# Indexer scores of two heads in two 64-row halves of the matrix engine, and one gate tile moved

## The chip, the cores and the metric

The kernel runs on one core of a Trainium2 chip. The metric is the device time of one execution in microseconds; three runs of the kernel before gave 1056.82, 1057.84 and 1059.62 us, median 1057.84. The engines are PE (matrix multiply), DVE (vector), ACT (scalar), POOL (general) and SP (issues DMAs). PE writes into PSUM; ACT and DVE read PSUM and write SBUF.

## The reference, cut to what matters

One layer of a streaming encoder, for 1024 prompt tokens and 32 sample tokens. One input projection gives, among others, the indexer's queries `qi` (8 heads of 64), its keys `ki` (64), its head weights `wi`, and two merge gates. The indexer scores every pair of query and key, and attention then uses only the best keys of each query:

```python
logits = jnp.einsum('bthd,bsd->bths', qi.astype(f32), ki_all.astype(f32)) * (IDX_DIM ** -0.5)
score = jnp.einsum('bth,bths->bts', wi.astype(f32), jax.nn.relu(logits))
...
top_val, top_idx = lax.top_k(score, n_sel)
```

Prompt queries see the keys up to the end of their 64-token chunk and select 256; sample queries see 512 cached keys and 32 new ones and select 136. All data are float32, and the scores decide which keys are taken, so they are computed in more than one pass of the matrix engine's rounded float32.

## The kernel before, in words

A float32 matrix is split into a high part (rounded to the engine's format) and a low part (the rest). A product then takes three passes: high by high, high by low and low by high. `mm3` (L270 to L272) does this for the projections.

**The stream.** All projections of 128 output columns are jobs of one stream `Z`. A job takes its weight tile (a DMA of 512 KB on SP), splits it in two (on ACT, DVE or POOL, as the job says), and issues 24 steps: three groups of 352 tokens by eight tiles of the contraction, each step one `mm3`. `run(us)` issues as many steps as fit into the given time at 0.483 us a step, so the order of PE's instructions is written by hand; a job's evacuation from PSUM follows its third group, in the selection some steps later (`LAG`). `gate_job(f)` is the job of gate tile f: its evacuation is a tanh on ACT (L707), and the result goes to DRAM with a DMA on SP. There are 16 gate tiles: 0 to NS-1 run at the start, NS to NI-1 behind the indexer's jobs, NI to 15 in the selection. With NS = NI = 7 none runs in the indexer.

**The indexer** (L1134 to L1194). Jobs: `ki`, then `qi0` to `qi3`, each of two heads. The evacuation of `qi` builds for each head a tile of 128 rows: 64 rows of the high part and 64 of the low part (L1127 to L1130), so that one pass over a key matrix that holds the keys twice gives high and low at once. For each of four pairs of heads, the seven query tiles (i = 2 to 7 of the prompt with 128(i+1) keys, and i = 8, the sample, with 32 queries and 544 keys), and each head: two passes (L1181 with the keys' high part, L1182 with the low part) in pieces of up to 512 columns into a PSUM tile `pss` of 1024 columns (two of these exist), a ReLU on ACT (L1184), and on DVE the weighted sum into `sco` (L1187, L1189). Then `run(0.25 + nk * FI)` issues stream steps. While pair j is scored, the stream projects `qi` of pair j+1; for the fourth pair it has nothing. The products of the merge's last gate row (L1109) come from a delay list in between. PE's order is by hand here; that of DVE, ACT, POOL and SP is found by the planner.

**The selection** (L1518 to L1621). 32 rounds of a binary search for the threshold of each query: ACT counts four of the tiles (L1513), DVE three (L1515), then DVE moves the thresholds (L1571, L1578). Each round issues `run(4.0)`. Behind the rounds the marks (L1585 to L1612, mostly DVE) write the masks `mb`, with further `run` calls. The stream has 16 jobs for this part: K, V and Q of the first pair of attention heads, gates 7 to 15 and `za0` to `za3`. The weight splits of the gates are on POOL here. `Z.until("za3")` at L1620 issues what is left of them. The order of DVE and ACT is by hand here too.

**The attention** follows: per item the products (L1349), maxima (L1355), exponentials (L1362), norm (L1367 to L1371), transposes (L1442 for rows, L1405 for the sample) and the output products, again with stream steps in between.

Of the kernel before, what the change touches and what calls it, by code (L numbers as in the profile page):

```python
# [7 lines left out]
F32 = mybir.dt.float32  # L8
F32R = mybir.dt.float32r
BF16 = mybir.dt.bfloat16  # L10
I32 = mybir.dt.int32
AF = mybir.ActivationFunctionType
ALU = mybir.AluOpType
# [4 lines left out]
NT = T + TS  # L18
# [5 lines left out]
NCH = 133  # L24
NST = 134
QT = [(i * 128, 128, 128 * (i + 1)) for i in range(8)]
NS, NI = 7, 7
WB = 5
SQ, HF, SM, GD, GH, NP, BL, HB, GL = 1, 4, 4, (1, 1, 0), 1, (0, 0, 2, 2), 1, 1, 0
TP = 1000  # L30
# [6 lines left out]
FI = 0.0007  # L37
# [20 lines left out]
def body(nc, tc, I, O, dbg=None):  # L58
# [3 lines left out]
    te, ve, se, ge, sp = nc.tensor, nc.vector, nc.scalar, nc.gpsimd, nc.sync  # L62

    def f32(ap):
        return ap.bitcast(F32)

    def split(h, l, src, heng, leng):
        if heng is se:
            se.copy(h, src)
        else:  # L70
            heng.tensor_copy(h, src)
        leng.tensor_sub(l, src, f32(h))  # L72
# [14 lines left out]
    def ps_x(tag, bufs, w=512):  # L87
        t = phase[1].tile([128, w], F32, tag=tag, bufs=bufs, name="ps" + tag)
        return t
# [14 lines left out]
    def ps_s(n="pss"):  # L104
        return ps_x("s", 2, 1024)
# [15 lines left out]
    def load_rows(xt, g, r, n, eng):  # L121
# [3 lines left out]
        if k < n:  # L125
# [30 lines left out]
                            op0=ALU.add, op1=ALU.mult)  # L156
# [109 lines left out]
    def wsplit(src, kt, n, pool=None, heng=None, leng=None):  # L266
        return wparts(wload(src, kt, n, pool), kt, n, pool, heng, leng)
# [52 lines left out]
    now, ve = ve, Later(ve, todo)  # L320
# [149 lines left out]
    for k in range(7):  # L470
        n = 1 << k
# [39 lines left out]
    ve = now  # L511
# [29 lines left out]
    ns = lambda n: slice(n * G3, (n + 1) * G3)  # L541
# [33 lines left out]
    class Stream:  # L575
# [77 lines left out]
        def run(self, us):  # L653
            self.credit += us / self.STEP
            while self.credit >= 1:
                if not self.step():
                    self.tick()
                self.credit -= 1
# [106 lines left out]
    for t in START.split():  # L765
# [6 lines left out]
        else:  # L772
            n = t.rstrip("0123456789")
# [210 lines left out]
    run = Z.run  # L984
# [77 lines left out]
    for q in range(4):  # L1062
# [4 lines left out]
        wh, wl = wsplit(w_glu[:, 128 * q:128 * q + 128], 4, 128, gp, leng=(ge, ve)[(YW >> q) & 1])  # L1067
        for n in range(3):
            c = ns(n)
            ps = ps_s("g")  # L1070
# [14 lines left out]
    sco = {i: scp.tile([128, 128 * (i + 1)], F32, name=f"sco{i}") for i in range(2, 8)}  # L1085
# [4 lines left out]
    ip = stI.enter_context(tc.tile_pool(name="ip", bufs=1, side="right", reuse_waits="tile"))  # L1090
# [28 lines left out]
    QS = {}  # L1119

    def qijob(j):
        def begin():
            qs = QS[j] = [ip.tile([128, NT], F32R, name=f"qis{e}", bufs=2) for e in range(2)]

            def ev(n, ps):
                c = ns(n)
                se.copy(qs[0][0:64, c], ps[0:64])  # L1127
                se.copy(qs[1][64:128, c], ps[64:128])
                ve.tensor_sub(qs[0][64:128, c], ps[0:64], f32(qs[0][0:64, c]))
                ve.tensor_sub(qs[1][0:64, c], ps[64:128], f32(qs[1][64:128, c]))  # L1130
            return ev
        return Job(f"qi{j}", wcol(C_QI + 128 * j), begin, heng=se, leng=ve)

# [18 lines left out]
    for k in range(9):  # L1152
        n = 128 if k < 8 else 32
# [9 lines left out]
    wi = cst.tile([128, 9, 8], F32)  # L1163
# [3 lines left out]
    kiH = ip.tile([128, 1568], F32R)  # L1167
    kiL = ip.tile([128, 1568], F32R)
    split(kiH, kiL, kid, ve, ge)
    for j in range(4):  # L1170
        Z.until(f"qi{j}")
        run(2.5)
        qs = QS[j]
        for i in range(2, 9):
            t0, m, k0, nk = (128 * i, 128, 0, 128 * (i + 1)) if i < 8 else (1024, 32, 1024, 544)
            for e in range(2):
                h = 2 * j + e
                ps = ps_s()
                for a in range(0, nk, 512):
                    b = min(nk, a + 512)  # L1180
                    te.matmul(ps[:m, a:b], qs[e][:, t0:t0 + m], kiH[:, k0 + a:k0 + b], start=True, stop=False)  # L1181
                    te.matmul(ps[:m, a:b], qs[e][:, t0:t0 + m], kiL[:, k0 + a:k0 + b], start=False, stop=True)  # L1182
                rl = ip.tile([128, 1024], F32, name="rl", bufs=2)
                se.activation(rl[:m, :nk], ps[:m, :nk], AF.Relu)  # L1184
                w = wi[:m, i, h:h + 1]
                if h == 0:
                    ve.tensor_scalar_mul(sco[i][:m, :nk], rl[:m, :nk], w)  # L1187
                else:
                    ve.scalar_tensor_tensor(sco[i][:m, :nk], rl[:m, :nk], w, sco[i][:m, :nk],  # L1189
                                            op0=ALU.mult, op1=ALU.add)  # L1190
                run(0.25 + nk * FI)
    for i in range(2, 8):
        ve.memset(sco[i][0:64, 128 * i + 64:128 * i + 128], -3.0e38)
    Z.flush()  # L1194
# [143 lines left out]
    class Soft:  # L1338

        def products(self, m, nk, mask, lhsT, rhs, np_=0):  # L1340
            self.m, self.nk, self.mask, self.np_ = m, nk, mask, np_
            self.P = at2.tile([128, 1024], F32, name="Sm", bufs=SM)
            self.S = []
            for a in range(0, nk, 512):
                c = slice(a, min(nk, a + 512))
                S = ps_x("s", 3)[:m, 0:c.stop - a]
                self.S.append((c, S))
                for t, r in enumerate(rhs):
                    te.matmul(S, lhsT, r[:, c], start=t == 0, stop=t == len(rhs) - 1)  # L1349
# [296 lines left out]
    for k in range(len(seq) + 3):  # L1646
        it = at(k)
        if k in first:
            p, begin = first[k]
            k0 = k  # L1650
# [9 lines left out]
        f = FA[p][e_] + FF * (it.i + 1 if it else 5)  # L1660
# [77 lines left out]
    for f in range(8):  # L1738
        wh, wl = wsplit(w_pa[:, 128 * f:128 * f + 128], 4, 128)
        tg = stg.tile([128, NT], F32, name="tgl", tag="stg")  # L1740
        sp.dma_start(tg, thD[8 + f])
        for n in range(3):
            ps = ps_x("m", 4)
# [63 lines left out]
    for rows in ((0, 1, 2), (8,), (3,), (4,), (5,), (6,), (LAST,)):  # L1807
        xts = {}
        for hcol in range(2):
            for i in rows:  # L1810
                n = 128 if i < 8 else 32
# [5 lines left out]
                for b_, c in enumerate(cols):  # L1817
                    ps = products(i, n, hcol, c)
# [4 lines left out]
                    if len(cols) == 2 and b_ == 0:  # L1823
                        ve.tensor_scalar(ss2[:n, 0, i:i + 1], ss2[:n, 0, i:i + 1], ss2[:n, 1, i:i + 1], None,
                                         op0=ALU.add)
# [53 lines left out]
```

## Time and profile before

| | |
|---|---|
| median of 3 runs | 1057.84 us (1056.82 to 1059.62) |
| profiled execution | 1056.18 us, of which span 1054.4 |
| PE busy | 994.8 us, 94% of the span |
| DVE busy | 761.5 us, 72% |
| ACT busy | 537.8 us, 51% |
| POOL busy | 260.2 us, 25% |
| granted PE clock, mean | 0.990 |
| score matmuls | L1181 and L1182, 96 each, 324.0 to 403.8 us |
| first projection of the selection | 404.19 us |
| first product of the attention | 609.84 us |

Times in rows are microseconds from the start of the span. A matmul's row shows its start, its length from first operand to last result, and its operands as rows by columns of the weights and shape of the stream; since matmuls are pipelined, the distance between two starts is what one costs, not its length. A row of a table of groups gives count, busy time and mean length in ns, then the idle time just before and what ended it.

### The profile page before, as it was taken

To read this page: it belongs to the slowest core of one execution; us is meant where nothing else is said; L and a number is where in the kernel's file an instruction comes from. 1 tells how busy PE (TensorE), PEld (TensorE's weight loads), DVE (VectorE), ACT (ScalarE), POOL (GpSimd) and SP (SyncE) were. 2 spreads that over 40 slices of the span, in tenths; PEclk is the share of its full clock that TensorE was granted. 3 is DMA by queue.
4 is the path that set the end of the run, shared out by engine and by line. 5 is a ranking of instruction groups with operands and counts; after the bars stand their busy time and mean duration, and the time that the engine had idled before them with its cause. 6 is when DMAs were issued, how large, how long until landed. Compare 5 with 4: busy or idle time off the path is not lost.

```text
span 1054.4 us, 17185 instructions
## 1 busy us (share of the span) xinstructions
PE 994.8 (94%) x6194; PEld 925.1 (88%) x6194; DVE 761.5 (72%) x1760; ACT 537.8 (51%) x1152; POOL 260.2 (25%) x471
## 2 busy tenths in 40 slices
PE   5999999998999989898999999999999999999997
PEld 3899999998889878898998998889898988998786
DVE  4669698994737789988889846756657776786534
ACT  3642245435435557768994346556556555443111
POOL 4200000313320231233313532333222231340000
PEclk9999999999899999999999999999999999999999
DMA  9923512317573110323232251242124622854311
GB/s 309 271 68 95 168 45 83 102 54 232 187 221 97 61 41 23 110 58 104 82 103 82 88 157 50 65 132 68 53 94 122 206 77 88 268 163 140 122 69 60
DMA packets 124177, 121.68 MB, mean 115 GB/s; under 512 B 14272, under 2 KB 104852, under 8 KB 124092
## 3 DMA queue, kind: packets, MB, share of 16 engines
q1 hardware_dynamic: 123712, 120.26, 37.2%
q8 instruction: 49, 0.80, 0.3%
q14 instruction: 36, 0.29, 0.1%
q10 hardware_dynamic: 220, 0.28, 0.1%
q0 software_dynamic: 160, 0.03, 0.0%
HBM read 85.64 MB, written 34.34 MB: 114 GB/s over the span
## 4 chain that ended last, share of the span: by engine, by line
PE 47%; DVE 10%; ACT 9%; issue 5%; POOL 0%; DMA 0%; POOLq 0%; ACTq 0%; DVEq 0%; SPq 0%
PE pz L270 6%; PE pz L272 6%; PE pz L271 6%; ACT junkb L1513 6%; PE pss L1349 3%; PE psm L1848 3%; PE psm L1850 3%; PE psm L1849 3%; PE pt L1442 2%; DVE junk L1515 2%; PE pspo L1461 2%; DVE sco L1189 1%; PE psm L270 1%; PE psm L272 1%; PE psm L271 1%
## 5 line engine op out<-in xcount | busy, mean ns | idle before, releaser
L270 PE MATMUL pz<-hH,wh 128*128 128x352 f32 (+1 forms) x776 | 261.5, 337 | 3.7 <-DVE zt L696 3.7
L272 PE MATMUL pz<-hH,wl 128*128 128x352 f32 (+1 forms) x776 | 251.5, 324 | 0.0
L271 PE MATMUL pz<-hL,wh 128*128 128x352 f32 (+1 forms) x776 | 251.5, 324 | 0.0
L263 POOL TENSOR_TENSOR wl<-raw,wh 128x256 fp32r<-128x256 f32 (+1 forms) x184 | 138.3, 779 | 135.5 <-ACT wh L258 128.1
L270 PEld LDWEIGHTS pz<-hH,wh 128*128 128x128 f32 (+1 forms) x776 | 145.9, 188 | 8.1 <-DVE zt L696 4.0
L271 PEld LDWEIGHTS pz<-hL,wh 128*128 128x128 f32 (+1 forms) x776 | 145.9, 188 | 1.3
L272 PEld LDWEIGHTS pz<-hH,wl 128*128 128x128 f32 (+1 forms) x776 | 145.7, 188 | 0.4
L1513 ACT ACTIVATE junkb<-sco,thr 128x896 bf16<-128x896 f32 (+3 forms) x128 | 103.6, 809 | 26.5 <-DVE thr L1578 20.1
L270 PE MATMUL pss<-hH,wh 128*128 128x352 f32 x304 | 102.4, 337 | 8.5 <-ACT tg L707 4.7
L272 PE MATMUL pss<-hH,wl 128*128 128x352 f32 x304 | 100.7, 331 | 1.2 <-POOL wl L263 1.2
L271 PE MATMUL pss<-hL,wh 128*128 128x352 f32 x304 | 100.5, 330 | 0.2 <-DVE hL L72 0.2
L1515 DVE TENSOR_SCALAR_CACHE_REDUCE junk<-sco,thr 128x1024 bf16<-128x1024 f32 (+2 forms) x96 | 96.9, 1010 | 2.4
L262 POOL CAST wh<-raw 128x256 fp32r<-128x256 f32 x88 | 35.0, 437 | 179.8 <-PE pz L271 164.2
L270 PEld LDWEIGHTS pss<-hH,wh 128*128 128x128 f32 x304 | 59.1, 194 | 11.6 <-POOL wh L262 5.3
L1445 DVE TENSOR_TENSOR PL<-pt,PH 128x512 fp32r<-128x512 f32 (+2 forms) x96 | 50.4, 552 | 25.8 <-ACT PH L1444 23.7
L1444 ACT CAST PH<-pt 128x512 fp32r<-128x512 f32 (+2 forms) x96 | 42.9, 482 | 46.1 <-PE pt L1442 43.4
L272 PEld LDWEIGHTS pss<-hH,wl 128*128 128x128 f32 x304 | 59.1, 194 | 1.7 <-POOL wl L263 1.7
L271 PEld LDWEIGHTS pss<-hL,wh 128*128 128x128 f32 x304 | 59.0, 194 | 0.4 <-DVE hL L72 0.4
L1362 ACT ACTIVATE Sm<-Sm,mx 128x128 f32<-128x128 f32 (+8 forms) x68 | 52.7, 775 | 9.2 <-DVE mx L1355 9.2
L1184 ACT ACTIVATE rl<-pss 128x384 f32<-128x384 f32 (+6 forms) x56 | 41.1, 738 | 29.8 <-PE pss L1182 21.5
L1189 DVE SCALAR_TENSOR_TENSOR sco<-rl,wi,sco 128x384 f32<-128x384 f32 (+6 forms) x49 | 46.4, 959 | 10.9 <-ACT rl L1184 10.0
L1850 PE MATMUL psm<-o,mL 128*128 128x512 f32 (+1 forms) x136 | 51.6, 381 | 0.0
(408 smaller groups left out, 2226.7 us busy)
## 6 DMA issues: line engine op xcount, KB each, us to landing
raw<-in_w_in SPq DMA_DIRECT2D x44, 512.0 KB
thD<-tg SPq DMA_DIRECT2D x16, 528.0 KB
tgl<-thD SPq DMA_DIRECT2D x16, 528.0 KB
wm<-in_w_mod SPq DMA_DIRECT2D x8, 1024.0 KB
rraw<-in_w_mod SPq DMA_DIRECT2D x4, 1024.0 KB
kd<-kd SPq DMA_DIRECT2D x32, 128.0 KB
xo<-in_x_prompt SPq DMA_DIRECT2D x8, 512.0 KB
rawo<-in_w_o SPq DMA_DIRECT2D x8, 512.0 KB
```

The costliest lines, as they stand in the source:

```text
L263: leng.tensor_sub(wl[:, c], raw[:, c], f32(wh[:, c]))
L270: te.matmul(ps, wh, xh, start=first, stop=False)
L271: te.matmul(ps, wh, xl, start=False, stop=False)
L272: te.matmul(ps, wl, xh, start=False, stop=last)
L1184: se.activation(rl[:m, :nk], ps[:m, :nk], AF.Relu)
L1189: ve.scalar_tensor_tensor(sco[i][:m, :nk], rl[:m, :nk], w, sco[i][:m, :nk], op0=ALU.mult, op1=ALU.add)
L1362: se.activation(P, P, AF.Exp, scale=-1.0, bias=self.mx, accum_out=self.rs)
L1444: se.copy(PH[:, b0:b1_, oc], src)
L1445: ve.tensor_sub(PL[:, b0:b1_, oc], src, f32(PH[:, b0:b1_, oc]))
L1513: se.activation(junkb[:m, :nk], x[:m], AF.Sign, bias=t, accum_out=cnt[:m, k:k + 1])
L1515: ve.tensor_scalar(junk[:m, :nk], x[:m], t, None, op0=ALU.is_lt, op1=ALU.add, accum_out=cnt[:m, k:k + 1])
L1850: te.matmul(ps, ml, wh, start=False, stop=last)
```

## The change

The queries are kept as a high and a low tile of two heads each (rows 0 to 63 are head 2j, rows 64 to 127 head 2j+1), split by one copy on ACT and one subtraction on DVE. A query tile is worked through in chunks of up to 512 columns (nk if it is at most 512, otherwise two halves). For each chunk there are three passes, high by high, low by high and high by low, and in each pass two matmuls: rows 0 to 63 into the first bank of the PSUM tile, rows 64 to 127 into the second. One ReLU takes both banks; DVE adds the two heads one after the other. `run` is called once a chunk, with the same sum over a pair of heads. NI becomes 8: gate tile 7 is projected behind `qi3`, with its splits on ACT and DVE, and no longer in the selection.

```diff
-NS, NI = 7, 7
+NS, NI = 7, 8
...
-            qs = QS[j] = [ip.tile([128, NT], F32R, name=f"qis{e}", bufs=2) for e in range(2)]
+            qh, ql = QS[j] = [ip.tile([128, NT], F32R, name=f"qi{h}", bufs=2) for h in "HL"]
 
             def ev(n, ps):
-                c = ns(n)
-                se.copy(qs[0][0:64, c], ps[0:64])
-                se.copy(qs[1][64:128, c], ps[64:128])
-                ve.tensor_sub(qs[0][64:128, c], ps[0:64], f32(qs[0][0:64, c]))
-                ve.tensor_sub(qs[1][0:64, c], ps[64:128], f32(qs[1][64:128, c]))
+                split(qh[:, ns(n)], ql[:, ns(n)], ps, se, ve)
...
-            for e in range(2):
-                h = 2 * j + e
-                ps = ps_s()
-                for a in range(0, nk, 512):
-                    b = min(nk, a + 512)
-                    te.matmul(ps[:m, a:b], qs[e][:, t0:t0 + m], kiH[:, k0 + a:k0 + b], start=True, stop=False)
-                    te.matmul(ps[:m, a:b], qs[e][:, t0:t0 + m], kiL[:, k0 + a:k0 + b], start=False, stop=True)
-                rl = ip.tile([128, 1024], F32, name="rl", bufs=2)
-                se.activation(rl[:m, :nk], ps[:m, :nk], AF.Relu)
...
-                run(0.25 + nk * FI)
+            w = nk if nk <= 512 else nk // 2
+            for a in range(0, nk, w):
+                ps = ps_s().rearrange("p (e c) -> p e c", e=2)[:m, :, 0:w]
+                kc = slice(k0 + a, k0 + a + w)
+                for x, (q_, k_) in enumerate(((qh, kiH), (ql, kiH), (qh, kiL))):
+                    for e in range(2):
+                        r = slice(64 * e, 64 * e + 64)
+                        te.matmul(ps[:, e], q_[r, t0:t0 + m], k_[r, kc], start=x == 0, stop=x == 2)
+                rl = ip.tile([128, 2, 512], F32, name="rl", bufs=2)[:m, :, 0:w]
+                se.activation(rl, ps, AF.Relu)
+                for e in range(2):
+                    h = 2 * j + e
+                    wh, dst = wi[:m, i, h:h + 1], sco[i][:m, a:a + w]
...
+                run((0.5 + 2 * nk * FI) * w / nk)
```

More of the change, by code (lines that the diff above doesn't have):

```diff
@@ L1172, in body @@
         run(2.5)
-        qs = QS[j]
+        qh, ql = QS[j]
         for i in range(2, 9):
             t0, m, k0, nk = (128 * i, 128, 0, 128 * (i + 1)) if i < 8 else (1024, 32, 1024, 544)
-            for e in range(2):
-                h = 2 * j + e
-                ps = ps_s()
-                for a in range(0, nk, 512):
-                    b = min(nk, a + 512)
-                    te.matmul(ps[:m, a:b], qs[e][:, t0:t0 + m], kiH[:, k0 + a:k0 + b], start=True, stop=False)
-                    te.matmul(ps[:m, a:b], qs[e][:, t0:t0 + m], kiL[:, k0 + a:k0 + b], start=False, stop=True)
-                rl = ip.tile([128, 1024], F32, name="rl", bufs=2)
[L1184 to L1190, printed above, removed]
-                run(0.25 + nk * FI)
+            w = nk if nk <= 512 else nk // 2
[11 more added lines that the diff above has]
+                    wh, dst = wi[:m, i, h:h + 1], sco[i][:m, a:a + w]
+                    if h == 0:
+                        ve.tensor_scalar_mul(dst, rl[:, e], wh)
+                    else:
+                        ve.scalar_tensor_tensor(dst, rl[:, e], wh, dst, op0=ALU.mult, op1=ALU.add)
+                run((0.5 + 2 * nk * FI) * w / nk)
     for i in range(2, 8):
```

## The prediction

> **What bounds the kernel now.** I read the page's totals first, then a table by stage cut where the PE's program changes: scores of the first three head pairs, scores of the fourth, the 32 rounds of the selection, the marks after them, the start of the attention.
>
> ```profile
> span 1054.4 us, 17185 instructions
> PE 994.8 (94%) x6194; PEld 925.1 (88%) x6194; DVE 761.5 (72%) x1760; ACT 537.8 (51%) x1152; POOL 260.2 (25%) x471
> ...
> PE 47%; DVE 10%; ACT 9%; issue 5%; POOL 0%; DMA 0%; POOLq 0%; ACTq 0%; DVEq 0%; SPq 0%
> ```
> ```profile
> 324.15:385.28 61.13, 60.94 (x355) 54.12 (x354) 47.47 (x64) 37.17 (x59) 9.35 (x12) 1.00 0.20 61
> 385.28:404.19 18.91, 15.32 (x64) 9.29 (x65) 18.50 (x27) 11.95 (x17) 5.76 (x7) 0.91 0.15 43
> 404.19:557.20 153.01, 142.02 (x872) 139.58 (x873) 134.33 (x326) 126.40 (x288) 43.08 (x81) 0.99 0.27 81
> 557.20:604.30 47.10, 45.05 (x270) 44.18 (x269) 44.01 (x68) 18.10 (x40) 23.58 (x26) 0.96 0.29 91
> 604.30:640.00 35.70, 34.57 (x226) 33.26 (x225) 17.64 (x52) 16.60 (x41) 10.05 (x21) 1.00 0.45 137
> ```
> The columns after the length are PE, weight loads, DVE, ACT and POOL busy, then the PE clock. PE has 94% of the span and the largest share of the chain, but not everywhere. Pairs 0 to 2 are PE's (60.94 of 61.13). Pair 3 is DVE's (18.50 of 18.91): no projection is left to run beside it, and weight loads wait for the ReLU to free PSUM:
>
> ```profile
> PEld pss L1181 <- ACT rl L1184: 7.9, 13, 1.4
> ```
> In the rounds DVE and ACT hand thresholds to each other and PE follows; in the marks DVE is full (44.01 of 47.10), and behind them PE still has projections to finish. A PE saving is worth its size only in the first stretch and from the marks on.
>
> **The change part by part.** First the PE's prices in the score stage: steps of the projection stream, and distance between starts by width.
>
> ```profile
> L270 PE MATMUL pz<-hH,wh 128*128 128x352 f32 x67 | 22.5, 335 | 0.0
> ```
> ```profile
> 324.15 0.34 PE L1181 MATMUL pss<-kiH,qis 128*128 128x384 f32 x1
> 324.33 0.34 PE L1182 MATMUL pss<-kiL,qis 128*128 128x384 f32 x1
> 324.50 0.32 PE L270 MATMUL pz<-hH,wh 128*128 128x352 f32 x1
> 324.66 0.32 PE L271 MATMUL pz<-hL,wh 128*128 128x352 f32 x1
> ...
> 331.54 0.32 PE L272 MATMUL pz<-hH,wl 128*128 128x352 f32 x1
> 331.79 1.07 PE L1109 MATMUL pg<-rraw,scP 128*32 128x512 f32 x8
> 332.78 0.43 PE L270 MATMUL pz<-hH,wh 128*128 128x352 f32 x1
> ...
> 340.01 0.39 PE L1181 MATMUL pss<-kiH,qis 128*128 128x512 f32 x1
> 340.24 0.40 PE L1182 MATMUL pss<-kiL,qis 128*128 128x512 f32 x1
> ```
> A 352-column matmul takes 0.16 us of PE, 384 columns 0.175, 512 columns 0.23, so width/2.4 ns and 16 ns on top. A step is three 352s: 0.483 us. The row product L1109 costs 1.1 us.
>
> *Scores, PE.* Stretch one holds 67 steps (32.4 us) and two L1109 (2.2 us); the other 26.5 us are three pairs of scores but for the sample tile of the last (about 1 us): **9.1 us a pair** for 48 matmuls. The new code has 12 chunks a pair (384, 512, and two each of 320, 384, 448, 512 and 272 columns), each with three passes by two halves. If the halves run side by side a pass costs one width: the twelve sum to 2.18 us, three passes to **6.5 us**. If not, 13.1.
>
> Do tiles of the array overlap? The trace has no two row halves. The nearest row is L1109: eight 512-column instructions into four column strips, each lasting about 0.6 us, in 0.99 us together. So strips overlap; I take that for row halves too.
>
> Each chunk is followed by at least one stream step, so PE goes from 128-row to 64-row tiles and back 48 times (about 46, the last ones lying together). The attention's sample item does this once a pair of heads, with five 64-row transposes; 72-row transposes are the comparison that stays in the full array:
>
> ```profile
> 754.29 0.32 PE L272 MATMUL pz<-hH,wl 128*128 128x352 f32 x1
> 754.54 0.51 PE L1405 MATMUL pt<-idf,Sm 64*128 64x64 f32 x5
> 754.99 0.43 PE L270 MATMUL pz<-hH,wh 128*128 128x352 f32 x1
> 755.25 0.32 PE L271 MATMUL pz<-hL,wh 128*128 128x352 f32 x1
> ```
> ```profile
> 313.17 0.32 PE L272 MATMUL pz<-hH,wl 128*128 128x352 f32 x1
> 313.33 0.42 PE L1158 MATMUL pt<-idf,zki 72*128 72x72 f32 x4
> 313.55 0.41 PE L270 MATMUL pz<-hH,wh 128*128 128x352 f32 x1
> 313.80 0.33 PE L271 MATMUL pz<-hL,wh 128*128 128x352 f32 x1
> ```
> From the matmul ahead to the second behind: 0.96 us with 64 rows, 0.63 with 72; a fifth transpose at 0.06 makes that 0.69. **A visit costs 0.27 us**, 0.09 of it at the entry (0.25 instead of 0.16). Bounds: 0 (the transposes are another data type) to 0.27; I take 0.27, since the entry wait precedes any difference in type. 46 visits: 12.4 us, more than the 4 x 2.6 = 10.4 us saved.
>
> The Trainium skill, TensorEngine Tiling (Array Packing), section Key Properties, says that a change of tiling mode drains the array; the rows agree. The same page's Theoretical Speedup gives up to 2x for a contraction of 64; by that alone the visits would be free and the pair 6.5 us.
>
> *Scores, DVE and ACT.*
>
> ```profile
> L1189 DVE SCALAR_TENSOR_TENSOR sco<-rl,wi,sco 128x896 f32<-128x896 f32 x7 | 8.1, 1158 | 1.7 <-ACT rl L1184 1.6
> ...
> L1130 DVE TENSOR_TENSOR qis<-pz,qis 64x352 fp32r<-64x352 f32 x11 | 5.8, 527 | 0.2
> ...
> L1189 DVE SCALAR_TENSOR_TENSOR sco<-rl,wi,sco 128x384 f32<-128x384 f32 x7 | 4.3, 613 | 1.3 <-ACT rl L1184 1.1
> ...
> L263 DVE TENSOR_TENSOR wl<-raw,wh 128x1024 fp32r<-128x1024 f32 x2 | 2.5, 1226 | 3.1 <-ACT wh L258 3.1
> ```
> From 384 to 896 columns: 1.064 ns a column and 0.2 us an instruction. DVE goes from 14 to 24 accumulations a pair, the columns unchanged: +2 us, +8 in all. Splitting qi takes one subtraction over 128 partitions instead of two over 64: -0.5 for each of nine evacuations inside the stage. The gate's weight split moves to DVE here: +1.2. DVE's 66.0 us of 80 (47.47 + 18.50) become about 70.7. ACT has 12 ReLUs a pair for 14 and half the qi casts; it gains the gate's cast and three tanh, and was busy 49 of 80, so nothing on the path. PSUM and SBUF tiles keep sizes and counts; a chunk still waits for the ReLU two chunks back, with the projection steps queued behind it on PE, and in stretch one that wait is almost nothing (0.19 us of PE not busy).
>
> *The gate tile.* 24 steps, 11.6 us of PE, leave the selection for pairs 2 and 3. Its weight load (SP), its two splits (POOL to ACT and DVE) and its store on SP go along; SP has nothing urgent behind it there (DMA share 0.15).
>
> *Sum for the stage.* 91 steps 43.9, three L1109 3.3, scores 26.1, visits 12.4: **85.7 us** from 324.15 to the first projection of the selection, which was 80.04 (404.19): **d = +5.7 us**.
>
> *Behind it.* By the code the rounds and marks ask for (128 + 46)/0.483 = 360 steps; the stream holds 16 tiles, 384. The remaining 24 run after the marks, and the gate's absence removes exactly these.
>
> ```profile
> 603.40 0.86 DVE L1594 TENSOR_TENSOR mb<-le,eq 32x544 bf16<-32x544 bf16 x1
> ```
> ```profile
> 609.84 0.22 PE L1349 MATMUL pss<-kH,qs 128*128 128x128 f32 x1
> 609.90 0.27 PE L1349 MATMUL pss<-kL,qs 128*128 128x128 f32 x1
> 610.01 0.38 PE L270 MATMUL pz<-hH,wh 128*128 128x352 f32 x1
> ...
> 616.42 0.27 PE L1442 MATMUL pt<-idf,Sm 128*128 128x128 f32 x1
> ```
> ```profile
> 610.60 0.52 DVE L696 SCALAR_TENSOR_TENSOR zt<-th,pz 128x352 f32<-128x352 f32 x1 [2.33 <-ACT th L695]
> 611.03 0.28 DVE L1355 CUSTOM_DVE_ANT_0 Sm<-pss,mb 128x128 f32<-128x128 f32 x1
> ...
> 612.97 0.54 DVE L1371 TENSOR_SCALAR Sm<-Sm,rs 128x128 f32<-128x128 f32 x1
> ```
> DVE ends the marks at 604.26 and starts the first maximum at 611.03, waiting for the last tile. With PE ahead, three 0.5 us evacuations move into the marks and one stays: the maximum at 606.3, 4.7 earlier. Its softmax is normalised at 613.51 and PE asks for it at 616.42: 2.9 more before PE waits. So PE's order moves by d - 11.6, DVE's lets it move by d - 7.6, and the later one decides: **d - 7.6 = -1.9 us**. The profiled execution took 1056.18 us (1.8 outside its span), 1.7 under the median 1057.84; from the median it is 1056.
>
> **The rivals.**
> 1. *The visits are cheap.* For it: the measured visit is of transposes. Then PE needs 73.3 us, but DVE's 70.7 with its waits becomes the bound; I take 75 to 77, d = -5 to -3, the end -13 to -11: 1045 to 1047, faster.
> 2. *Weights are not loaded ahead in halves.* The pair 609.90 to 610.01 shows 0.11 us where 128 columns of stream need 0.07: a load takes 0.11. Six loads in a row per chunk would be 0.66, over the matmuls by 0.9 us a pair: d = +9.3, end +1.7. If each half's load also waits for its own matmul, 0.11 a pass, 16 us in all, with the 0.09 entry in place of 0.27: d = +13.2, end +5.6, 1063; with 0.27 a visit besides, 1072. For it: the five transposes take 0.45 us, 0.09 each. The Trainium skill, TensorE: Matmul & The Clock Gate, Part 3, has such a rule: loads pass running matmuls only where the row groups differ. No row here shows two row groups.
> 3. *The halves do not overlap* (slower): 13.1 us a pair, 26 us more, d = +32, end +24; with free visits +12: 1070 to 1082. It decides from 1.9 + 3.2 = 5 us, so as soon as a fifth of the overlap is lost. Against it: L1109.
>
> **How the numbers follow.** Forecast (1053 to 1060) 0.41; rival 1 0.27; rival 2 beyond it 0.18; rival 3 0.12; other 0.02. About 3.2 us (0.3%) is what a measurement can tell from no change. Faster is rival 1 and 0.09 of the forecast: 0.36. Slower is rival 3, 0.12 of rival 2 and 0.02 of the forecast: 0.26. The rest, 0.38, is no change. The range takes in rival 1 and most of rival 2: 1046 to 1069.
>
> **What would show it.** The two matmuls of a pass starting within 0.05 us of each other and a pass repeating after 0.15 to 0.23 us: overlap. The first stream matmul after a chunk at 0.25 us or more, and a late first load: visits. The first projection of the selection at about 410; no stream left behind the marks; the first maximum at about 612. I am wrong if PE waits on DVE in all four pairs, or if the planner orders the ReLUs behind the gate's tanh.

## The result: 1071.6 us, 1.25% slower

The changed kernel takes 1071.6 us (median of 4 runs, 1069.98 to 1072.22); the kernel before, beside it, 1058.07 us (1056.82 to 1059.62). The ratio is 1.0125, 95% interval 1.0107 to 1.0143. The forecast was 1056 us, the range 1046 to 1069. The profiled execution took 1071.97 us with a span of 1070.2.

The page of the changed kernel: span, busy times, shares of the chain by engine.

```profile
span 1070.2 us, 17326 instructions
PE 1003.7 (94%) x6290; PEld 921.4 (86%) x6290; DVE 763.1 (71%) x1789; ACT 532.1 (50%) x1133; POOL 255.8 (24%) x463
...
PE 47%; DVE 11%; ACT 11%; issue 3%; POOL 1%; DMA 0%; ACTq 0%; POOLq 0%; DVEq 0%; SPq 0%
```

The totals say little: PE is 9 us busier, the other engines are within 6 us of before, and the mean granted clock is 0.974 for 0.990. The table by stage (after the length: PE, weight loads, DVE, ACT, POOL busy, then the PE clock) tells more. The rows are scores of pairs 0 to 2, scores of pair 3, rounds, marks, start of the attention.

```profile
325.82:395.28 69.46, 69.46 (x443) 49.63 (x442) 49.56 (x84) 34.21 (x46) 5.05 (x7) 1.00 0.18 54
395.28:419.80 24.52, 21.58 (x147) 14.84 (x145) 20.78 (x35) 12.87 (x19) 8.07 (x12) 0.96 0.14 44
419.80:576.30 156.50, 145.45 (x861) 142.88 (x862) 135.31 (x332) 126.70 (x288) 41.67 (x77) 0.95 0.28 84
576.30:623.50 47.20, 40.96 (x257) 40.65 (x255) 44.15 (x68) 16.59 (x38) 27.34 (x30) 0.96 0.32 103
623.50:656.00 32.50, 30.87 (x186) 29.55 (x187) 16.26 (x53) 15.74 (x38) 5.27 (x13) 0.91 0.34 101
```

The scores take 93.98 us instead of 80.04, and in pairs 0 to 2 PE is never idle (69.46 of 69.46): a gain for DVE or ACT is worth nothing there. In the marks PE is less busy than before, since the gate tile is gone, but neither rounds nor marks are shorter.

The 15.8 us of span split like this: 1.67 lie ahead of the first score (325.82 against 324.15; that point scatters from 323.9 to 328.9 over the kernels run here, and the change doesn't touch what precedes it), 13.94 in the scores, -1.01 from there to the attention's first row transposes (631.02 against 616.42), 1.20 behind them. The forecast was 0, +5.7, -7.6, 0. So two terms failed: the scores by 8, the selection by 6.6.

**The scores.** PE's timeline at the first chunk (start, length, line, operands; `x2` groups two neighbouring rows of one form, here both halves of a pass):

```profile
325.57 0.32 PE L272 MATMUL pz<-hH,wl 128*128 128x352 f32 x1
325.82 0.44 PE L1179 MATMUL pss<-kiH,qiH 64*128 64x384 f32 x2
326.10 0.34 PE L1179 MATMUL pss<-kiH,qiL 64*128 64x384 f32 x2
326.28 0.34 PE L1179 MATMUL pss<-kiL,qiH 64*128 64x384 f32 x2
326.55 0.43 PE L270 MATMUL pz<-hH,wh 128*128 128x352 f32 x1
326.81 0.32 PE L271 MATMUL pz<-hL,wh 128*128 128x352 f32 x1
```

From the second pass on, both matmuls of a pass lie in one row no longer than one alone (0.34), and the next pass starts 0.18 us later, one width. So the halves overlap. The price is at the borders: 0.25 into the chunk (0.16 within the stream), 0.28 from the first pass to the second (0.18 to the third), 0.27 from the last pass to the stream, 0.26 from that matmul to the next (0.16). From 325.57 to 326.81 are 1.24 us; less two 352s (0.32) and three widths (0.525) remain **0.39 us a visit**, not 0.27. Chunks of 512, 320 and 448 columns give 0.41, 0.39 and 0.40, those of the sample tile (32 columns of weights) 0.30. There are 44 visits (stretches of score matmuls between stream rows), eight of them of the sample tile: some 17 us. With 43.9 of stream, 3.3 of L1109, 26.1 of overlapped scores and the waits below (3.0) that is some 93 of the 93.98 us.

The weight loads of the same chunk (PEld) show what a visit is made of:

```profile
325.82 0.19 PEld L1179 LDWEIGHTS pss<-kiH,qiH 64*128 64x128 f32 x2 [0.22 <-issue]
325.93 0.19 PEld L1179 LDWEIGHTS pss<-kiH,qiL 64*128 64x128 f32 x2
...
326.54 0.19 PEld L270 LDWEIGHTS pz<-hH,wh 128*128 128x128 f32 x1 [0.25 <-issue]
326.65 0.19 PEld L271 LDWEIGHTS pz<-hL,wh 128*128 128x128 f32 x1
```

Within the stream a load starts about 0.16 us ahead of its matmul (L272's at 325.41 for 325.57). At both borders it starts only with its matmul (325.82, 326.54), and the next load follows 0.11 later. So each border costs twice: 0.09 until its first matmul starts, and 0.10 more until the second, about one load. In the sample tile's visits, whose weights have 32 columns, only the step from the first pass to the second is shorter: 0.15 for a width of 0.13. By these rows that part goes with the size of the weights. What holds the first load back isn't shown.

PE's waits in the scores (total us, times, longest):

```profile
PE pss L1179 <- ACT rl L1181: 1.9, 2, 1.5
PE pss L270 <- POOL qsm L1270: 1.1, 1, 1.1
```

**The selection.** PE's waits from 595 to 635 us, then the rows of PE and DVE around it:

```profile
PE pss L1347 <- DVE zt L696: 6.7, 1, 6.7
```
```profile
614.94 0.22 PE L1347 MATMUL pss<-kH,qs 128*128 128x128 f32 x1
...
616.93 0.32 PE L272 MATMUL pz<-hH,wl 128*128 128x352 f32 x1
624.00 0.58 PE L1347 MATMUL pss<-kH,qs 128*128 128x256 f32 x1 [6.75 <-DVE zt L696]
...
624.60 0.49 PE L270 MATMUL pz<-hH,wh 128*128 128x352 f32 x1
624.89 0.49 PE L271 MATMUL pz<-hL,wh 128*128 128x352 f32 x1
...
629.59 0.32 PE L270 MATMUL pz<-hH,wh 128*128 128x352 f32 x1
629.74 0.32 PE L271 MATMUL pz<-hL,wh 128*128 128x352 f32 x1
```
```profile
623.09 0.43 DVE L1592 TENSOR_TENSOR mb<-le,eq 32x544 bf16<-32x544 bf16 x1
623.45 0.50 DVE L696 SCALAR_TENSOR_TENSOR zt<-th,pss 128x352 f32<-128x352 f32 x1
623.88 0.50 DVE L696 SCALAR_TENSOR_TENSOR zt<-th,pz 128x352 f32<-128x352 f32 x1
624.31 0.27 DVE L1353 CUSTOM_DVE_ANT_0 Sm<-pss,mb 128x128 f32<-128x128 f32 x1
```

PE is ahead, as forecast: it issues the attention's first product at 614.94, 8.6 us before the last mark ends (623.52). But it can't issue the second. The attention's score tiles lie where the selection's wide tiles lay (`ps_z` takes the `s` tiles of the pool that `ps_phase` closes), and the last outputs of `za3` sit in them until DVE evacuates them, behind the last mark. Then PE runs at half clock (granted 0.50 from 624.0 to 629.3): 352 columns every 0.29 us instead of 0.16 for 15 matmuls, some 2 us more.

Of the 6.6 us by which the selection missed its forecast, 4.2 lie behind the first maximum, where these stops are: from there to the transposes are 6.71 us, and the forecast had 2.5 (5.39 less 2.9). The other 2.4 lie ahead of it. DVE's first mark, before and after:

```profile
557.57 0.75 DVE L1585 TENSOR_SCALAR le<-sco,thr 128x1024 bf16<-128x1024 f32 x1
```
```profile
575.23 0.76 DVE L1583 TENSOR_SCALAR le<-sco,thr 128x1024 bf16<-128x1024 f32 x1
```

It comes 155.43 us behind the first projection of the selection; in the kernel before it was 153.38. So the rounds, which the forecast left as they were, take 2.05 us more. DVE is no busier there (134.24 us for 134.63); it waits longer, 1.6 us for 0.5 on a DMA of K and 10.7 for 9.8 on ACT's counts. Why isn't shown. The marks are 1.6 us longer, as forecast for three evacuations that move into them.

### The profile page after: what moved, and what is told of

Its sections match the earlier page's. It is cut to its first block, busy times and chain, and to the rows that moved or that the text cites. A ratio compares the mean times of both kernels' runs of the same rounds, so it can differ in the third digit from the quotient of the medians.

```text
span 1070.2 us, 17326 instructions
## 1 busy us (share of the span) xinstructions
PE 1003.7 (94%) x6290; PEld 921.4 (86%) x6290; DVE 763.1 (71%) x1789; ACT 532.1 (50%) x1133; POOL 255.8 (24%) x463
## 4 chain that ended last, share of the span: by engine, by line
PE 47%; DVE 11%; ACT 11%; issue 3%; POOL 1%; DMA 0%; ACTq 0%; POOLq 0%; DVEq 0%; SPq 0%
PE pz L270 7%; ACT junkb L1511 7%; PE pz L271 6%; PE pz L272 6%; PE pss L1179 3%; PE pss L1347 3%; PE psm L1846 3%; PE psm L1848 2%; PE psm L1847 2%; PE pt L1440 2%; PE pspo L1459 2%; PE pspo L1457 1%; PE psm L270 1%; PE psm L272 1%; PE psm L271 1%
## 5 line engine op out<-in xcount | busy, mean ns | idle before, releaser
L270 PE MATMUL pz<-hH,wh 128*128 128x352 f32 (+1 forms) x792 | 271.4, 343 | 3.9 <-DVE zt L696 3.9
L272 PE MATMUL pz<-hH,wl 128*128 128x352 f32 (+1 forms) x792 | 257.5, 325 | 0.0
L271 PE MATMUL pz<-hL,wh 128*128 128x352 f32 (+1 forms) x792 | 257.5, 325 | 0.0
L263 POOL TENSOR_TENSOR wl<-raw,wh 128x256 fp32r<-128x256 f32 (+1 forms) x180 | 132.5, 764 | 145.9 <-ACT wh L258 138.6
L270 PEld LDWEIGHTS pz<-hH,wh 128*128 128x128 f32 (+1 forms) x792 | 149.6, 189 | 19.5 <-issue 12.6
L271 PEld LDWEIGHTS pz<-hL,wh 128*128 128x128 f32 (+1 forms) x792 | 149.8, 189 | 0.9
L272 PEld LDWEIGHTS pz<-hH,wl 128*128 128x128 f32 (+1 forms) x792 | 149.5, 189 | 0.4
L270 PE MATMUL pss<-hH,wh 128*128 128x352 f32 x288 | 99.2, 344 | 10.3 <-POOL wl L263 3.6
L272 PE MATMUL pss<-hH,wl 128*128 128x352 f32 x288 | 96.8, 336 | 0.2 <-POOL wl L263 0.2
L270 PEld LDWEIGHTS pss<-hH,wh 128*128 128x128 f32 x288 | 57.5, 200 | 13.4 <-POOL wl L263 3.9
L1188 DVE SCALAR_TENSOR_TENSOR sco<-rl,wi,sco 128x384 f32<-128x384 f32 (+4 forms) x84 | 55.9, 675 | 17.3 <-ACT rl L1181 16.0
L1181 ACT ACTIVATE rl<-pss 128x768 f32<-128x768 f32 (+4 forms) x48 | 39.9, 833 | 45.8 <-PE pss L1179 31.2
L1360 ACT ACTIVATE Sm<-Sm,mx 128x128 f32<-128x128 f32 (+8 forms) x68 | 52.7, 775 | 10.7 <-DVE mx L1353 10.7
L272 PEld LDWEIGHTS pss<-hH,wl 128*128 128x128 f32 x288 | 57.2, 199 | 0.5 <-POOL wl L263 0.5
L1353 DVE CUSTOM_DVE_ANT_0 Sm<-pss,mb 128x512 f32<-128x512 f32 (+4 forms) x68 | 40.2, 591 | 16.7 <-PE pss L1347 16.0
```

Of the source, the lines that this page charges most:

```text
L263: leng.tensor_sub(wl[:, c], raw[:, c], f32(wh[:, c]))
L270: te.matmul(ps, wh, xh, start=first, stop=False)
L271: te.matmul(ps, wh, xl, start=False, stop=False)
L272: te.matmul(ps, wl, xh, start=False, stop=last)
L1181: se.activation(rl, ps, AF.Relu)
L1188: ve.scalar_tensor_tensor(dst, rl[:, e], wh, dst, op0=ALU.mult, op1=ALU.add)
```

## The experiments

Theory T: (1) the halves overlap wholly; (2) a visit costs 0.39 us of a PE that is the bound; (3) the gate's work costs the scores more than it brings the selection, because held PSUM tiles stop PE there. It says nothing of the longer rounds. The rivals stand in the expectations. Positions are of the profiled execution, the ratio is to the kernel before:

| kernel | first score | first projection of the selection | first maximum | first row transposes | median us | ratio, 95% interval |
|---|---|---|---|---|---|---|
| before | 324.15 | 404.19 | 611.03 | 616.42 | 1058.07 | |
| changed | 325.82 | 419.80 | 624.31 | 631.02 | 1071.6 | 1.0125, 1.0107 to 1.0143 |
| e1 halves only | 326.68 | 416.41 | 623.98 | 629.37 | 1067.75 | 1.0087, 1.0063 to 1.0111 |
| e2 gate only | 324.29 | 410.23 | 613.71 | 619.72 | 1060.73 | 1.0020, 1.0006 to 1.0035 |
| e6 gate, MS | 324.47 | 410.40 | 614.96 | 616.35 | 1055.99 | 0.9968, 0.9945 to 0.9991 |
| e12 changed, MS | 325.92 | 419.88 | 624.78 | 626.16 | 1065.54 | 1.0077, 1.0064 to 1.0090 |

### e1 and e2: each part of the change alone

```diff
-NS, NI = 7, 8      # e1, from the changed kernel
+NS, NI = 7, 7
-NS, NI = 7, 7      # e2, from the kernel before
+NS, NI = 7, 8
```

> The two halves and three passes stay; the gate tile is put back into the selection (NS, NI = 7, 7). Theory T (each of the 46 switches between 64-row tiles and the 128-row stream costs about 0.39 us of PE, and the gate's 11.6 us of PE bring only some 2 to 3 us in the selection): the stage is 24 steps shorter than in the changed kernel, so from the first score matmul to the first projection of the selection about 82 to 84 us; the whole about 1062 to 1068 us. Rival R2 (it is the gate move that costs the time, the halves are about neutral): about 1058 us.

> The kernel before with only the gate tile moved (NS, NI = 7, 8). Theory T: the score stage about 5 us longer than the 80.04 us of before (it has idle PE that takes half of the 11.6 us), the selection 2 to 5 us shorter: 1057 to 1062 us. Rival R2 (the gate move costs the time): about 1070 us. If the selection gets 7 us shorter or more, the explanation by tiles that stay held is wrong, and it would be 1053 us or less.

Both are slower than before, e1 by 0.87%, e2 by 0.20%; together 1.07% of the 1.25%. R2 falls: most is the halves'. The score stage of e1 and of e2, and e1's waits of PE in it:

```profile
326.68:416.41 89.73, 80.91 (x514) 55.40 (x514) 68.05 (x118) 46.08 (x63) 12.93 (x18) 0.94 0.17 51
```
```profile
324.29:410.23 85.94, 84.44 (x490) 73.88 (x490) 68.04 (x91) 51.32 (x79) 13.29 (x15) 1.00 0.19 56
```
```profile
PE pss L1179 <- ACT rl L1181: 8.0, 8, 2.9
```

T had e1's stage at 82 to 84 us; it is 89.7. Without the gate's steps nothing runs beside the scores of pair 3, PE waits 8.0 us for the ReLUs, and the clock falls (0.94 over the stage). So moving the gate fills a gap that the halves make larger: its 11.6 us of PE lengthen the stage by 4.3 us in the changed kernel (93.98 against 89.73) and by 5.9 in the kernel before (85.94 against 80.04). In e2 the way from the first projection of the selection to the first row transposes shrinks by 2.7 us only (209.49 against 212.23), so the move alone loses.

### e3, e7, e8: the number of visits

```diff
-                run((0.5 + 2 * nk * FI) * w / nk)
+            run(0.5 + 2 * nk * FI)                          # e3: behind the last chunk of a tile

                     for e in range(2): ...                  # e7: also behind the first pass
+                    if x == 0:
+                        run((0.25 + nk * FI) * w / nk)
-                run((0.5 + 2 * nk * FI) * w / nk)
+                run((0.25 + nk * FI) * w / nk)

-                run((0.5 + 2 * nk * FI) * w / nk)
+                if i != 2 and b_ == nk:                     # e8: every two chunks; b_ = a + w
+                    run(0.5 + 2 * nk * FI + (0.5 + 768 * FI if i == 3 else 0))
```
(e8 also has MS = 0.0095, as e6 below.)

> The changed kernel, with the stream's turn taken once a query tile, behind its last chunk, in place of once a chunk: the same matmuls, ReLUs and accumulations, the same number of stream steps, but 28 visits to the 64-row tiles for 48. Theory T: 20 visits less at 0.39 us, the score stage about 7.8 us shorter than 94.0, the whole about 1064 us; some of it may come back as PE waiting for ReLUs between the two chunks. Rival R3 (the 24 accumulations a pair make DVE the bound of the stage): nothing gained, about 1071 us.

> The changed kernel, with each chunk's stream steps taken in two parts, one between the first and the second pass and one behind the third: 96 visits to the 64-row tiles for 48, all else the same. Theory T (0.39 us a visit): 48 x 0.39 = 18.7 us more in a stage that PE bounds, about 1089 us (1085 to 1092). Rival R6 (what e3 gained came from the grouping of the ReLUs and the stream, the switch itself costs the 0.27 us of the prediction or less): at most 13 us more, 1084 us or less; with a free switch about 1072 us.

> The changed kernel with a visit for every two chunks (24 for 48) and MS 0.0095. Theory T: from e3's 1062.3, four visits less at 0.39 us (1.6 us) and the 2 to 4 us that e6 is to gain: 1057 to 1059 us, the kernel before within its noise. If e6's step fails, about 1061 us; if PE waits for the ReLUs inside the longer visits, 1062 or more.

Measured: e3 1062.32 us (ratio 1.0047, 1.0031 to 1.0063), e7 1082.87 (1.0219, 1.0170 to 1.0269), e8 1058.48 (0.9998, 0.9975 to 1.0020). The score stage of each, in this order, each row from its own kernel's table:

```profile
324.85:412.21 87.36, 84.38 (x586) 65.67 (x586) 68.51 (x119) 46.40 (x66) 12.33 (x16) 0.99 0.18 55
```
```profile
326.64:432.31 105.67, 102.46 (x587) 63.88 (x586) 69.40 (x118) 47.10 (x64) 12.65 (x18) 1.00 0.15 46
```
```profile
328.92:414.66 85.74, 82.75 (x586) 65.95 (x586) 68.36 (x119) 45.93 (x66) 12.33 (x16) 0.99 0.19 56
```

The expectations count calls of `run`; where a call's credit is less than one step no visit ends. By the rows there are 27 visits in e3, 75 in e7, 23 in e8 and 44 in the changed kernel. So 31 more visits cost 11.69 us (105.67 less 93.98), 0.38 each; 17 fewer save 6.62, 0.39 each; 21 fewer save 8.24, 0.39 each. The price is the same from both sides and agrees with the rows. e7's total missed its range (1085 to 1092) because 17 of its 48 added calls make no visit. That total lies where R6 put it (1084 or less), but R6 reached it by 48 visits at 0.27; 31 visits at 0.27 would be 8.4 us, and the stage grew by 11.69, so R6 falls. R3 falls: with the same accumulations e3's DVE is about as busy as in the changed kernel (68.51 us for 70.34) and the stage is 6.6 us shorter. e8 came out as forecast (1057 to 1059), but its stage, 85.74 us, only draws level with the old scores beside the same gate tile (e2: 85.94).

### e4 and e5: do the halves overlap?

```diff
-                for x, (q_, k_) in enumerate(((qh, kiH), (ql, kiH), (qh, kiL))):
-                    for e in range(2):
+                for e in range(2):                          # e4: head by head
+                    for x, (q_, k_) in enumerate(((qh, kiH), (ql, kiH), (qh, kiL))):

-                        r = slice(64 * e, 64 * e + 64)
+                        r = slice(0, 64)                    # e5: both in the upper half
```

> The changed kernel with the six matmuls of a chunk ordered head by head (three passes of the upper half, then three of the lower) in place of pass by pass. Theory T (the two halves overlap wholly now): only the third pass of one head and the first of the other can still overlap, so a chunk takes five widths for three; over four pairs some 2 x 2.2 us x 4 = 17 us more, about 1089 us. Rival R4 (the halves hardly overlap even now): no change, about 1071 us.

> The changed kernel, with both matmuls of a pass reading the same 64 rows (the upper half; head 2j is computed twice and head 2j+1 left out). All else as in the changed kernel. Theory T (the halves overlap wholly, and head by head made no difference because a matmul of the other half is started past waiting ones): here nothing can overlap, so a chunk takes six widths for three, 6.5 us a pair more, 26 us in all on a PE that is the bound: about 1092 to 1102 us. Rival R4 (the halves don't overlap in the changed kernel either): no change, about 1071 us.

e4 took 1071.1 us (1.0122, 1.0101 to 1.0142): the number that R4 gave. Taken alone it would have buried the right theory. Its trace, and then that of e5, each for one chunk of 512 columns with the stream matmul behind it:

```profile
325.98 0.50 PE L1179 MATMUL pss<-kiH,qiH 64*128 64x512 f32 x2
326.32 0.39 PE L1179 MATMUL pss<-kiH,qiL 64*128 64x512 f32 x2
326.55 0.39 PE L1179 MATMUL pss<-kiL,qiH 64*128 64x512 f32 x2
326.87 0.44 PE L270 MATMUL pz<-hH,wh 128*128 128x352 f32 x1
```
```profile
326.83 0.72 PE L1179 MATMUL pss<-kiH,qiH 64*128 64x512 f32 x2
327.39 0.63 PE L1179 MATMUL pss<-kiH,qiL 64*128 64x512 f32 x2
327.86 0.63 PE L1179 MATMUL pss<-kiL,qiH 64*128 64x512 f32 x2
328.42 0.44 PE L270 MATMUL pz<-hH,wh 128*128 128x352 f32 x1
```

In e4 the two heads still run side by side, pass by pass, although the lower half's first matmul is issued behind all three of the upper half: 0.89 us a chunk. What failed is the premise that PE starts matmuls in the order of issue. In e5 both matmuls want the same 64 rows; a pass repeats after 0.47 us, two widths, and the chunk takes 1.59. The whole took 1093.88 us (1.0320, 1.0272 to 1.0367), inside T's range, and the stage:

```profile
324.44:442.29 117.85, 116.54 (x586) 87.56 (x586) 70.32 (x119) 47.32 (x64) 12.27 (x18) 0.99 0.14 41
```

23.9 us longer, where the forecast had 26 for the loss of the overlap. R4 falls.

### e6, e9 to e12: what stops PE behind the marks

```diff
-LAG, RS, MS, RM, RB = 4.0, 4.0, 0.008, 14.0, 1
+LAG, RS, MS, RM, RB = 4.0, 4.0, 0.0095, 14.0, 1     # e6, e10: on e2; e9: on before; e12: on the changed kernel
+LAG, RS, MS, RM, RB = 4.0, 4.0, 0.011, 14.0, 1      # e11: on e2
```

MS sets how much of the stream is issued among the marks; a larger one brings `za3`'s evacuations forward.

> The kernel before with the gate tile moved (as in e2) and MS 0.0095 for 0.008: the stream is drawn out earlier during the marks, so that the evacuations of the selection's last tiles are issued among the marks and their PSUM tiles are free when the attention's score products want them. Theory T (the gate's gain in the selection was lost because these evacuations, behind the marks, held the PSUM tiles of the attention's first products): PE's wait of 6 to 7 us there goes, and PE reaches the attention's first transposes 2 to 4 us sooner: 1057 to 1059 us for e2's 1060.7. Rival R5 (VectorE alone sets that point, its work is the same): no gain, about 1060.7 us.

> The kernel before with MS 0.0095 alone, the gate tile left in the selection. Theory T (e6 gained because PE had room and waited for held PSUM tiles; with the gate tile in the selection PE is the bound there and waits for nothing): no gain, 1056 to 1060 us. Rival R7 (the larger MS is a gain by itself, whatever the gate does): 4 to 5 us less than before, about 1053 us.

> The kernel of e6 once more, with more rounds, to see whether it beats the kernel before: 1054 to 1057 us, a ratio of about 0.997.

> As e6 with MS 0.011. In e6 VectorE goes from the last mark to the first maximum without a gap and PE still waits 3.5 us for one evacuation among the last marks. Theory T: that wait is shorter, but VectorE's own work now sets the first transposes (1.4 us behind the first maximum), so no more than 1 us is gained: 1054.5 to 1057 us.

> The changed kernel with MS 0.0095 alone. Theory T: the same held PSUM tiles cost the changed kernel what they cost e2, so it gains what e6 gained on e2 (4.7 us): about 1067 us (1065.5 to 1068.5). If the score stage had hidden something of it, less.

PE's waits behind the marks, first in e2, then in e6, and e6's PE rows behind the longer of them:

```profile
PE pss L1349 <- DVE zt L696: 6.8, 1, 6.8
```
```profile
PE pz L270 <- DVE zt L696: 3.5, 1, 3.5
PE pt L1442 <- DVE Sm L1371: 1.2, 1, 1.2
```
```profile
612.58 0.43 PE L270 MATMUL pz<-hH,wh 128*128 128x352 f32 x1 [3.53 <-DVE zt L696]
...
613.52 0.32 PE L270 MATMUL pz<-hH,wh 128*128 128x352 f32 x1
613.68 0.32 PE L271 MATMUL pz<-hL,wh 128*128 128x352 f32 x1
```
And DVE of e6 from its last evacuation to the first maximum:

```profile
612.01 0.52 DVE L696 SCALAR_TENSOR_TENSOR zt<-th,pz 128x352 f32<-128x352 f32 x1 [0.81 <-ACT th L695]
...
614.60 0.43 DVE L1594 TENSOR_TENSOR mb<-le,eq 32x544 bf16<-32x544 bf16 x1
614.96 0.27 DVE L1355 CUSTOM_DVE_ANT_0 Sm<-pss,mb 128x128 f32<-128x128 f32 x1
```

With no evacuation behind the marks, the products are ready when the last mask is: the transposes follow the first maximum by 1.39 us for 6.01, PE keeps its clock (352 columns every 0.16 us behind the 3.5 us wait), and e6 takes 1055.99 us for e2's 1060.73. The same edit brings the changed kernel from 1071.6 to 1065.54 (ratio 1.0125 to 1.0077), the transposes 1.38 us behind the maximum. On the kernel before (e9) it brings nothing: 1058.53 us, 1.0013 (0.9996 to 1.0029); R7 falls. R5 falls too: the same work on DVE, and PE reaches the transposes sooner. (In e2 the granted clock was 0.50 from 613.4 to 617.2, so part of what e6 gains is the clock that the long wait cost.) So part of the gate's gain was there and was held up by those tiles.

It isn't all of it: in e6 the last mark ends 202.4 us behind DVE's first count of the selection, before 198.6. The evacuations that moved among the marks (before has five behind the last mark, e6 none, 0.5 us each) make some 2.5 of these 3.8 us; the rest stays open. e11 missed: 1058.81 us (1.0022, 1.0011 to 1.0033) for at most 1057. Its marks end another 2.6 us later, and PE, out of work, waits for DVE:

```profile
PE pt L1442 <- DVE Sm L1371: 7.5, 1, 7.5
```

e10, the repeat of e6, took 1057.36 us (0.9990, 0.9976 to 1.0004), just above the forecast of 1054 to 1057. With e6's 0.9968 that is a gain of 0 to 0.3% on the kernel before, too small to claim. No version that was run clearly beats it.

## Why the prediction was wrong, point by point

- **Overlap of the halves: right.** 6.5 us a pair was forecast; the rows repeat by one width, and e5 shows that losing the overlap costs 23.9 us. The Trainium skill, TensorEngine Tiling (Array Packing), Theoretical Speedup, allows up to 2x for a contraction of 64; the trace agrees for the passes (0.23 us for two 512s against 0.47 in one half), and the borders ate the gain.
- **The price of a visit: the first step that failed.** Forecast 0.27, measured 0.38 to 0.39. That each visit costs PE time at its borders was right (0.25 at the entry), the size was not. The step was "0.96 less 0.69": the 72-row transposes taken as the comparison carry a border themselves. In the rows shown there, the L270 behind them starts the next matmul 0.25 us later (613.55 to 613.80), where the stream needs 0.16: a penalty of 0.09 was subtracted from a penalty. The same 0.96 less plain work, two 352s (0.32) and five transposes at 0.055 (0.28), is 0.36; that leaves 0.03, for which the rows show no single place. With 44 visits for 46 the term is some 17 us instead of 12.4.
- **Rival 1, cheap visits: wrong**, by e3, e7 and e8 alike. **Rival 2, loads not hidden within the halves: wrong** but for the first pass: all later passes repeat by their width, in e5 even within the same half. A load of about 0.11 is paid once a border, not once a pass. That its last sum (1072) meets the measured time is luck, as is the lower end of rival 3 (1070). The Trainium skill, TensorE: Matmul & The Clock Gate, Part 3, lets weight loads overlap running matmuls only where the row groups differ; e5's 0.47 us for two 512s in one row group differs from that, and the measurement decides. **Rival 3: wrong** by e5.
- **DVE and ACT: right.** DVE busy 70.34 us in the stage (49.56 and 20.78), forecast 70.7, and not on the path in pairs 0 to 2. What was missing is a term of 3.0 us for PE's waits in the last pair, though the view of before showed that pair to be DVE's.
- **The gate in the selection: the second step that failed.** "PE's order moves by d - 11.6, DVE's by d - 7.6." The first maximum came 2.3 us earlier, counted from the first projection of the selection (204.51 against 206.84), not 4.7, mostly because the rounds took 2.05 us more, a term that the sum put at nothing; why they did stays open. The 2.9 us of slack up to the transposes turned into a loss of 1.3 (6.71 against 5.39), and that is the larger part. The sum took PE as free to run ahead once its queue was shorter. It didn't ask in which PSUM tiles the products lie and who empties them: the last evacuations of `za3`, of which two stand on DVE behind the marks. Here the next limit, once work was taken from PE, was a tile that DVE held; e6, e10 and e12 show 3 to 5.5 us of it (0.30 to 0.52% in the ratios). The term came to -1.0 us for -7.6.
- **The bound** was read rightly (PE in the scores, DVE in the marks), as was the sign of the stage; the range missed by 2.6 us. No single term left it: the visits (some 5 us), the waits in the last pair (3.0) and the selection (6.6) did it together.

## What to carry to other kernels

Splitting the array in halves pays by the pass and costs by the switch: here a visit costs 0.39 us, and a chunk of 512 columns saves one pass, 0.23 us, so one chunk a visit loses. Two chunks a visit (e8) drew level in the score stage and no more; more than two were not run. When a price is worked out as a difference of two sequences, work each out against plain work first; the reference may carry the same cost. When PE's queue is shortened, look up which PSUM tiles the work behind it needs and where their evacuation stands in the other engines' order.

## What was not expected of the hardware

- PE doesn't start matmuls of different row halves in the order of issue: in e4 the fourth of six starts with the first (one row, `x2`, 0.50 us long), past two that wait for their half. The Trainium skill, TensorE: Matmul & The Clock Gate, Part 2, Step-by-step, says that matmuls stay in program order; the rows of e4 differ.
- After a wait of 6.75 us PE ran at half clock for 5 us (0.29 us for 352 columns, granted clock 0.50), behind a wait of 3.53 us in e6 it didn't (0.16 us). The Trainium skill, TensorE: Matmul & The Clock Gate, Part 1, What's actually happening, gives an idle window of about 3.4 us for the drop to half speed; the longer wait agrees, the shorter one is at that border.
